# First mixture of experts: each expert's products in two halves of 32 slots, the second under a test

## The chip, the cores and the metric

The kernel runs on one core of a Trainium2 chip. The metric is the time of one execution on the device in microseconds (us), the median of three runs.

## The reference

The model has two layers over 256 context rows and 256 latent rows of width 1024. Each layer ends with a two-level mixture of 32 gated experts (width 512, float32). A token goes to two experts of one group of eight:

```python
grp = jnp.argmax(lg, axis=-1).astype(jnp.int32)
...
p_in, e_in = lax.top_k(jax.nn.softmax(le, axis=-1), MOE_TOP_K)
gates = gw * p_in / jnp.sum(p_in, axis=-1, keepdims=True)
eidx = grp[:, None] * MOE_PER_GROUP + e_in.astype(jnp.int32)
...
return (jax.nn.silu(xe @ w_gate[e]) * (xe @ w_up[e])) @ w_down[e]
```

The first layer's mixture takes all 512 rows, so 1024 pairs of a token and an expert, 32 per expert in the mean; the second layer's takes the 256 latent rows alone. For the inputs that are given, the reference's routing sends these numbers of tokens to the experts 0 to 31 of the first mixture: 41, 58, 58, 85, 39, 26, 53, 60, 17, 25, 20, 41, 18, 15, 44, 32, 17, 24, 27, 38, 29, 17, 18, 6, 30, 28, 21, 14, 45, 26, 24, 28. The kernel may not depend on them: any routing has to come out right.

## The kernel before, in words

Two functions compute a mixture: `experts()` (line 1895 on) the first, `narrow()` (line 2225 on) the second. In both, weights come through `Stream`, a ring of tiles of 128x2048 float32, 1 MB each: `take()` hands out the next tile, `give(n)` releases n and issues the next n loads on SP's queue (line 150). An expert has six tiles: gate and up for two halves of the inner dimension, then two of the down product. The ring has 11 slots in the first mixture (`RING`, line 24, the first two parts) and 16 in the second.

`experts()` goes through the experts in blocks of four (`GB`). The router makes a position for every pair; `onehot()` turns those of a block into selection matrices with 64 slots (`SLOTS`) per expert, and `gather()` brings the block's tokens into `XG`, one column per slot. Then for each expert e:

- `stage1` (line 1956), gate and up product: 16 pairs of matmuls into the bank b3. Gate uses 64 columns of the array, up the other 64, each with 512 columns of weights that stream past:

```python
for j in range(2):
    nc.tensor.matmul(ps[64 * j:64 * j + 64], xe(k), w[j][:, k % 4], start=k == 0, stop=k == 7)
```

- the test `tc.If(flag(e) > 0)` (flag line 2110, test line 2194): `shared()` (line 2042) is a further block for tokens beyond an expert's 64. Under expert 31's test lie also expert 0's and `others()`, a loop over blocks that could take any number of tokens beyond. The flags are computed on VectorE (`extra`) and read into a register by each engine.
- `hidden` (line 1958): silu of the gate half on ScalarE (line 1960), product with up half and gate weight on VectorE (line 1961).
- `products(e - 1)`: the down product of the expert before (`stage2`, line 1977), again two groups of 64 columns by 512, into b4; `parts` (line 1980) evacuates it in two pieces of 64x512, rounded by ScalarE (line 1984) and the rest by VectorE (line 1985). Then `give(6)`.
- scatter of finished pairs (`scatter`, line 1996; PE at line 2000), the gather of the next block, `hidden_t` (line 1966; four transposes at line 1969 and a copy), and for even e the turned selection matrix of a pair.

The profile counts two matmuls for each float32 one in the code. The order of the work is the order of this code on every engine: nothing reorders it. The second mixture (`narrow()`) has the same steps with 32 slots per expert (`NARROW`), gate and up product in four groups of 32 array columns by 256 columns of weights (line 2284), down product alike (line 2301), evacuation in four pieces (line 2449), a test of its own (line 2494), and down tiles loaded as two pieces of rows.

Of the kernel before, what the change touches and what calls it, by code (L numbers as in the profile page):

```python
# [206 lines left out]
class Kernel:  # L207
# [1404 lines left out]
    def moe_tiles(self, NT):  # L1612
# [8 lines left out]
            extra=mp.tile([128, NE + 1 if NT > 2 else 3 * NE + 1], I32, name="extra"))  # L1621
# [195 lines left out]
    def bookkeeping(self, gp, lgg, mg, m1, m2, ohg, masked, chosen, oh1, oh2, slots, blocks):  # L1817
# [33 lines left out]
        nc.vector.tensor_reduce(over, counts.rearrange("p t e -> p e t"), axis=AX.X, op=ALU.add)  # L1851
        nc.vector.tensor_scalar(over, over, float(slots), 0.0, op0=ALU.subtract, op1=ALU.max)
# [19 lines left out]
        flags = gp.tile([128, extra.shape[1]], F32, name="flags")  # L1872
# [13 lines left out]
        at = 0 if blocks > 1 else NE - 1  # L1886
        for v in (more, flags):
            nc.vector.tensor_tensor(flags[:, at:at + 1], flags[:, at:at + 1], v[:, 0:1], op=ALU.max)
# [7 lines left out]
    def experts(self, L, x, seg, bookkeeping, ending):  # L1896

        nc, tc, c, stream, I = self.nc, self.tc, self.c, self.stream, self.I
# [4 lines left out]
        GB = 4  # L1903
        with ExitStack() as st:
# [4 lines left out]

            place = cycle([(wp, "xg"), (self.xp, "x01")] if L else [(wp, "xg"), (wp, "xh")])  # L1910
# [28 lines left out]
            def gates_of(b):  # L1939

                g2 = self.m["gate2"]
                ps = pp.tile([128, GB // 2, 2, 2], F32, name="b2")
                for i in range(GB // 2):
                    for t in range(NT):
                        nc.tensor.matmul(ps[:, i].rearrange("p h e -> p (h e)"), OH[b][:, t, 2 * i:2 * i + 2].rearrange("p e s -> p (e s)"),
                                         g2[:, :, t, b * GB + 2 * i:b * GB + 2 * i + 2],
                                         start=i == 0 and t == 0, stop=t == NT - 1, skip_group_check=True)
# [10 lines left out]
            def hidden(ps, gs):  # L1958
                sg, hs = low[:, 0:FE], low[:, FE:].rearrange("p (k q) -> p k q", k=4)
                nc.scalar.activation(sg[64:128], ps[0:64], AF.Silu)  # L1960
                nc.vector.scalar_tensor_tensor(  # L1961
                    hs[64:128].rearrange("s k q -> s q k"), ps[64:128].rearrange("s (q k) -> s q k", k=4), gs,
                    sg[64:128].rearrange("s (q k) -> s q k", k=4), op0=ALU.mult, op1=ALU.mult)
                return hs

            def hidden_t(hs, ht, tag=dict(name="b2")):
                pt = pp.tile([128, 4, SLOTS], F32, **tag)
                for k in range(4):
                    nc.tensor.transpose(pt[:, k], hs[64:128, k], c["ident"][64:128, 64:128])
                ht = ht.rearrange("p (k s) -> p k s", k=4)  # L1970
# [3 lines left out]
            def stage2(ps, ht, w, half):  # L1974
                for k in range(2 * half, 2 * half + 2):
                    for j in range(2):
                        nc.tensor.matmul(ps[64 * j:64 * j + 64], ht[:, k], w[:, k % 2, 512 * j:512 * j + 512],  # L1977
                                         start=k == 0, stop=k == 3)

            def parts(ps, yh, yl):  # L1980

                for j in range(2):
                    pj = ps[64 * j:64 * j + 64]
                    nc.scalar.copy(out=yh[:, j], in_=pj)  # L1984
                    nc.vector.tensor_tensor(yl[:, j], pj, yh[:, j].bitcast(F32), op=ALU.subtract)  # L1985
# [56 lines left out]
            def shared(e, w):  # L2042

                ps = pp.tile([128, FE], F32, name="b7")
                for half in range(2):
                    stage1(ps, lambda k: xx[:, k], w(2 * half, 2), half)
                ht = hidden_t(hidden(ps, gx[64:128, e:e + 1]), wp.tile([128, 512], F32, name="tmp")[:, 0:256], dict(name="b7"))
                ps = pp.tile([128, 512], F32, name="b7")
                for half in range(2):
                    stage2(ps, ht, w(4 + half, 1)[0], half)  # L2050
# [3 lines left out]
            def back():  # L2054

                a, b = (xg(F32R) for i in range(2))
                oht = a[:, 0:T].rearrange("p (t q) -> p t q", t=NT)
                yh, yl = (v.rearrange("p (j f) -> p j f", j=2) for v in (a[:, T:T + 1024], b[:, 0:1024]))
                nc.scalar.copy(out=yh[0:64], in_=yx)
                nc.vector.tensor_tensor(yl[0:64], yx, yh[0:64].bitcast(F32), op=ALU.subtract)  # L2060
                turned(lambda t: ohx[:, t], SLOTS, oht)
                scatter([(oht, yh, SLOTS), (oht, yl, SLOTS)], pieces)
# [17 lines left out]
            def last_scatter(py, Y, OT):  # L2080

                bank = self.bank_of(("b0", "b1", "b5", "b6", "b7"))

                def scaled(s):
                    for i in range(2):
                        a = slice(64 * i, 64 * i + 64)
                        nc.vector.tensor_tensor(Y[s][64:128, i], py[a], g2[s][a, 512 * i:512 * i + 512], op=ALU.mult)

                scaled(segs[0])
                for t, j in pieces:  # L2090
                    s = seg[t]
                    if (t, j) == (0, 1) and segs[1:]:
                        scaled(segs[1])
                    ps = bank([128, 512])
                    nc.tensor.matmul(ps, OT[:, t].bitcast(F32), Y[s][:, j], start=True, stop=True)
# [4 lines left out]
            def load(e):  # L2100
                def get(at, n):
                    ws = [xg(F32) for i in range(n)]
                    for w, loads in zip(ws, self.expert_loads(L, e)[at:at + n]):
                        for view, src in loads:
                            nc.sync.dma_start(out=view(w), in_=src)
                    return [w.rearrange("p (k f) -> p k f", k=4 if at < 4 else 2) for w in ws]
                return get
# [4 lines left out]
            def others():  # L2112

                n = flag(NE, self.most_blocks(NT, 1))
                with tc.If(n > 0):
# [3 lines left out]
                    with tc.For_i(0, n, 1):  # L2119
# [3 lines left out]
                        for e in range(NE):  # L2123
                            shared(e, load(e))
                        back()
                    nc.gpsimd.memset(yx, 0.0)
# [4 lines left out]
            rest = bookkeeping(Carved(wp.tile([128, 1024], F32, name="yh")))  # L2131
# [5 lines left out]
            late = None  # L2137
            def products(e):

                ps = pp.tile([128, 512], F32, name="b4")  # L2140
                for half in range(2):
                    stage2(ps, ht[e], w[e][4 + half], half)
                if e + 1 < NE:
                    if e % 2 == 0:
                        y[e // 2] = [wp.tile([128, 2, 512], F32R, name=m) for m in ("yh", "yl")]
                    a = slice(64 * (e % 2), 64 * (e % 2) + 64)
                    parts(ps, *(v[a] for v in y[e // 2]))
# [437 lines left out]
```

## Time and profile before

| what | us |
|---|---|
| three runs | 1886.25, 1885.99, 1883.76 |
| median | 1885.99 |
| profiled execution, its own time | 1889.25 |
| its span in the trace | 1887.4 |
| PE (TensorE matmul) busy | 1636.5 (87%) |
| DVE (VectorE) busy | 817.7 (43%) |
| ACT (ScalarE) busy | 446.9 (24%) |
| POOL (GpSimd) busy | 139.3 (7%) |

The mean granted clock of TensorE over the span is 0.922 of full speed. The shares of busy time are means over stages with different limits; a change in one stage has to be read from that stage. SP issues the loads, and "PEq" or "SPq" is the sequencer of an engine, "PEld" TensorE's loading of weights beside its matmuls. PE, DVE and the like name the engines below. "w" is a tile of the ring, "b" a bank of the accumulator.

### The profile page before, as it was taken

How to read it: one execution, taken by the hardware profiler on the slowest of the kernel's cores; microseconds unless marked ns; L12 is line 12 of the kernel's file. 1: busy time of each engine (PE TensorE's matmuls, PEld its weight loads, DVE VectorE, ACT ScalarE, POOL GpSimd, SP SyncE). 2: the span in 40 equal slices, each digit the busy share in tenths (PEclk: the TensorE clock that was granted, in tenths of full speed). 3: DMA queues.
4: the chain of work that ended last, by engine and by line, in shares of the span. 5: the costliest groups of instructions: out<-in, count | busy, mean ns of one | idle time of the engine just before them, and what ended most of it. 6: DMA issues, size and time to landing. Idle time of an engine off the chain costs nothing. (4 is left out here: it accounts for less than half of the span.)

```text
span 1887.4 us, 31596 instructions
## 1 busy us (share of the span) xinstructions
PE 1636.5 (87%) x12946; PEld 930.7 (49%) x12946; DVE 817.7 (43%) x1622; ACT 446.9 (24%) x945; POOL 139.3 (7%) x169
## 2 busy tenths in 40 slices
PE   5988999989998999999999987999977887766665
PEld 2754556454775444444444434889743433332222
DVE  2455434644358245455555458564642212211112
ACT  3442222421113111111111114454421111111011
POOL 1111000102115000000000004100110000000000
PEclk8998988989898999999999998999999889888887
DMA  9266300643144879999999981522889998999992
GB/s 317 81 217 209 113 24 23 227 159 120 55 145 179 352 287 380 404 389 389 373 400 388 380 343 45 171 71 73 326 319 414 415 415 335 414 415 414 415 415 107
DMA packets 127284, 505.76 MB, mean 268 GB/s; under 512 B 11317, under 2 KB 38945, under 8 KB 85986
## 3 DMA queue, kind: packets, MB, share of 16 engines
q1 hardware_dynamic: 120946, 493.96, 67.4%
q0 software_dynamic: 3488, 8.26, 1.3%
q8 instruction: 144, 2.36, 0.5%
q10 hardware_dynamic: 2640, 0.65, 0.2%
q14 instruction: 66, 0.54, 0.1%
HBM read 501.73 MB, written 1.10 MB: 266 GB/s over the span
## 5 line engine op out<-in xcount | busy, mean ns | idle before, releaser
L1977 PE MATMUL b<-w,ht 128*64 128x512 f32 x512 | 118.5, 603 | 9.2 <-PEq L2194 8.3
L2002 DVE TENSOR_TENSOR tmp<-b,g 128x512 f32<-128x512 f32 x128 | 87.6, 686 | 70.1 <-PE b L2000 69.2
L1956 PE MATMUL b<-w,xh 128*64 128x512 f32 x512 | 117.0, 598 | 0.0
L1956 PE MATMUL b<-w,xg 128*64 128x512 f32 x512 | 116.9, 598 | 0.0
L2284 PE MATMUL b<-w,x 128*32 128x256 f32 x1024 | 80.3, 439 | 27.0 <-DMA w<-moe_w_up 21.5
L2301 PE MATMUL b<-w,ht 128*32 128x256 f32 x1024 | 78.3, 450 | 18.2 <-ACT ht L2296 13.3
L2284 PE MATMUL b<-w,xg 128*32 128x256 f32 x1024 | 73.7, 412 | 22.5 <-DMA w<-moe_w_up 13.6
L2004 DVE TENSOR_TENSOR x<-x,tmp 128x512 f32<-128x512 f32 x124 | 90.1, 726 | 4.3
L1985 DVE TENSOR_TENSOR yl<-b,yh 64x512 fp32r<-64x512 f32 x62 | 42.7, 688 | 101.7 <-ACT yh L1984 101.7
L2449 DVE COPY y<-b 32x256 f32<-32x256 f32 x62 | 25.9, 418 | 134.5 <-PE b L2301 121.2
L1977 PEld LDWEIGHTS b<-w,ht 128*64 128x64 f32 x512 | 41.5, 138 | 84.4 <-issue 69.1
L2289 DVE SCALAR_TENSOR_TENSOR low<-b,gs,low 64x256 f32<-64x256 f32 x32 | 15.7, 490 | 151.8 <-ACT low L2288 151.8
L1960 ACT ACTIVATE low<-b 64x512 f32<-64x512 f32 x33 | 19.4, 589 | 254.0 <-PEq L2194 232.8
L2284 PEld LDWEIGHTS b<-w,x 128*32 128x32 f32 x1024 | 37.4, 123 | 67.5 <-DMA w<-moe_w_up 29.8
L1984 ACT CAST yh<-b 64x512 fp32r<-64x512 f32 x62 | 36.0, 581 | 128.0 <-PE b L1977 104.7
L1961 DVE SCALAR_TENSOR_TENSOR low<-b,gs,low 64x512 f32<-64x512 f32 x32 | 36.1, 1127 | 67.3 <-ACT low L1960 67.3
L1956 PEld LDWEIGHTS b<-w,xh 128*64 128x64 f32 x512 | 34.3, 136 | 62.2 <-issue 61.7
L1956 PEld LDWEIGHTS b<-w,xg 128*64 128x64 f32 x512 | 33.9, 136 | 62.3 <-issue 61.3
L2284 PEld LDWEIGHTS b<-w,xg 128*32 128x32 f32 x1024 | 35.7, 119 | 57.1 <-DMA w<-moe_w_up 18.4
L2288 ACT ACTIVATE low<-b 64x256 f32<-64x256 f32 (+1 forms) x36 | 14.4, 400 | 204.5 <-PEq L2494 105.6
L2000 PE MATMUL b<-yh,oht 128*128 128x512 f32 (+1 forms) x128 | 57.9, 452 | 4.0 <-DVE tmp L2002 4.0
L1374 PE MATMUL b<-w,hH 128*128 128x256 f32 x320 | 60.9, 291 | 0.0
(865 smaller groups left out, 3101.3 us busy)
## 6 DMA issues: line engine op xcount, KB each, us to landing
w<-moe_w_gate SPq DMA_DIRECT2D x128, 1024.0 KB
w<-moe_w_up SPq DMA_DIRECT2D x128, 1024.0 KB
w<-moe_w_down SPq DMA_DIRECT2D x128, 1024.0 KB
w<-ada_w SPq DMA_DIRECT2D x48, 1024.0 KB
w<-od_w_in SPq DMA_DIRECT2D x12, 1024.0 KB
w<-ev_w_in SPq DMA_DIRECT2D x8, 1024.0 KB
w<-ev_w_out SPq DMA_DIRECT2D x5, 1024.0 KB
w<-od_w_out SPq DMA_DIRECT2D x4, 1024.0 KB
```

The costliest lines, as they stand in the source:

```text
L1374: nc.tensor.matmul(ps[:, t], l[:, k, T], r[:, k], start=t == 0 and k == 0 and i == 0, stop=k == 7 and i == 2, skip_group_check=True)
L1956: nc.tensor.matmul(ps[64 * j:64 * j + 64], xe(k), w[j][:, k % 4], start=k == 0, stop=k == 7)
L1961: nc.vector.scalar_tensor_tensor(hs[64:128].rearrange("s k q -> s q k"), ps[64:128].rearrange("s (q k) -> s q k", k=4), gs, sg[64:128].rea ...
L1977: nc.tensor.matmul(ps[64 * j:64 * j + 64], ht[:, k], w[:, k % 2, 512 * j:512 * j + 512], start=k == 0, stop=k == 3)
L1984: nc.scalar.copy(out=yh[:, j], in_=pj)
L1985: nc.vector.tensor_tensor(yl[:, j], pj, yh[:, j].bitcast(F32), op=ALU.subtract)
L2000: nc.tensor.matmul(ps, ohT[0:n, t], y[0:n, j], start=i == 0, stop=i == len(parts) - 1)
L2002: nc.vector.tensor_tensor(tmp, ps, g2[seg[t]][:, 512 * j:512 * j + 512], op=ALU.mult)
L2004: (nc.gpsimd if j in aside else nc.vector).tensor_tensor(xs, xs, tmp, op=ALU.add)
L2284: nc.tensor.matmul(ps[groups[j]], xe(k), w[j // 2][:, k % 4, 256 * (j % 2):256 * (j % 2) + 256], start=k == 0, stop=k == 7, skip_group_che ...
L2301: nc.tensor.matmul(ps[groups[j]], ht[:, k % 2, S * (k // 2):S * (k // 2) + S], w[:, k % 2, 256 * j:256 * j + 256], start=k == 0, stop=k == ...
L2449: (nc.scalar.copy if j % 2 else nc.vector.tensor_copy)(out=out, in_=ps[groups[j]])
```

## The change

Only the first mixture changes. `XG` and the selection matrices keep 64 slots per expert. Gate, up and down products are made for the first 32 slots of an expert in the four-group form of the second mixture. A second flag per expert, whether it has more than 32 tokens, stands in `extra`. Under a test of it the gate and up product of slots 32 to 63 are made into bank b7, then, nested, the old test and `shared()`; at the expert's end, under a second test of the same flag, comes that half's down product. The rows of a pair of experts are now two fixed pairs of tiles, set to zero at the start, since a half that is left out writes nothing. `give(6)` becomes `give(4)` behind the first test and `give(2)` behind the down product. Expert 0's test and `others()` move from expert 31 to expert 29. The down tiles come in two pieces of 4 KB per partition, as in the second mixture.

The diff, cut to its core:

```diff
-            [rows(I["moe_w_down"][L, e], 4, half) if L == 0 else
-             [(lambda w: w.rearrange("p (k f) -> p k f", k=2), I["moe_w_down"][L, e].rearrange("(k p) f -> p k f", k=4)[:, 2 * half:2 * half + 2])]
+            [[(lambda w: w.rearrange("p (k f) -> p k f", k=2), I["moe_w_down"][L, e].rearrange("(k p) f -> p k f", k=4)[:, 2 * half:2 * half + 2])]
              for half in range(2)]
...
+            nc.vector.tensor_scalar(flags[:, NE + 1:], over, NARROW + 0.5, None, op0=ALU.is_gt)
...
-                GS[b] = wp.tile([128, GB], F32, name="gs")
+                GS[b] = wp.tile([128, 2, GB], F32, name="gs")
                 for j in range(2):
-                    nc.vector.tensor_reduce(GS[b][64:128, j::2], ps[64 * j:64 * j + 64, :, :, j], axis=AX.X, op=ALU.add)
+                    for u in range(2):
+                        for h in groups[2:]:
+                            nc.vector.tensor_reduce(GS[b][h, u, j::2], ps[groups[2 * j + u], :, :, j], axis=AX.X, op=ALU.add)
...
                 for k in (4 * half + i for i in ks):
-                    for j in range(2):
-                        nc.tensor.matmul(ps[64 * j:64 * j + 64], xe(k), w[j][:, k % 4], start=k == 0, stop=k == 7)
+                    for j in range(4):
+                        nc.tensor.matmul(ps[groups[j]], xe(k), w[j // 2][:, k % 4, 256 * (j % 2):256 * (j % 2) + 256], start=k == 0, stop=k == 7,
+                                         skip_group_check=True)
...
+            def parts(ps, rows, yh, yl):
+
+                for j in range(4):
+                    out = slice(256 * (j % 2), 256 * (j % 2) + 256)
+                    nc.scalar.copy(out=yh[rows, j // 2, out], in_=ps[groups[j]])
+                    nc.vector.tensor_tensor(yl[rows, j // 2, out], ps[groups[j]], yh[rows, j // 2, out].bitcast(F32), op=ALU.subtract)
...
+            rows = [[wp.tile([128, 2, 512], F32R, name=f"y{m}{i}", bufs=1) for m in "hl"] for i in range(2)]
+            nc.gpsimd.memset(low, 0.0)
+            for y in sum(rows, []):
+                nc.scalar.copy(out=y.rearrange("p j f -> p (j f)"), in_=low)
...
+                if e == NE - 3:
+
+                    with tc.If(flag(0) > 0):
+                        shared(0, loaded(0))
+                        others()
                 for half in range(2) if e else ():
-                    stage1(ps, xe, w[e][2 * half:2 * half + 2], half)
+                    stage1(ps, xe(0), w[e][2 * half:2 * half + 2], half)
...
+                hs = hidden(ps, gs(0), low[64:128, 0:256], low[64:128, 256:512])
+                with tc.If(flag(NE + 1 + e) > 0):
+                    ps = pp.tile([128, 256], F32, name="b7")
+                    for half in range(2):
+                        stage1(ps, xe(1), w[e][2 * half:2 * half + 2], half)
+                    hidden(ps, gs(1), low[64:128, 512:768], low[64:128, 768:1024])
+                    if e:
+                        with tc.If(flag(e) > 0):
+                            shared(e, resident(w[e]))
+                if not end:
+                    stream.give(4)
                 if e:
-                    with tc.If(flag(e) > 0):
-                        shared(e, lambda at, n: w[e][at:at + n])
-                        if e + 1 == NE:
-                            with tc.If(flag(0) > 0):
-                                shared(0, load(0))
-                            others()
-                hs = hidden(ps, GS[b][64:128, r:r + 1])
-                if e:
-                    products(e - 1)
-                    if e + 1 < NE:
-                        stream.give(6)
+                    ps = second(e - 1, ht.pop(e - 1), w.pop(e - 1))
+                    parts(ps, *part_rows(e - 1, 0))
+                    if not end:
+                        stream.give(2)
                     scatter(rows_of(late) if todo else (), todo[n:])
...
+                with tc.If(flag(NE + 1 + e) > 0):
+                    ps = second(e, hidden_t(low[64:128, 768:1024], wp.tile([128, 512], F32, name="tmp")[:, 0:128].rearrange("p (k s) -> p k s", k=2)),
+                                w[e])
+                    if end:
+                        for s in segs:
+                            scaled(ps, s, 1)
+                    else:
+                        parts(ps, *part_rows(e, 1))
```

How the instructions stand on the engines. First PE around one expert's test, before. L1956 is the gate and up product, here its second half of 8 matmuls; the rows between the compare and the branches are `shared()`, and the L1977 row behind them is the down product of the expert before.

```order
L1956 MATMUL b_6668<-w,xg 64x512 x8
L2110 TENSOR_LOAD extra
L2194 COMPARE_AND_BRANCH
L1956 MATMUL b_6712<-w,xx 64x512 x16
L1969 MATMUL b_6732<-const_ident,low 128x64 x4
L1977 MATMUL b_6738<-w,tmp 64x512 x8
L2194 UNCONDITIONAL_BRANCH x2
L1977 MATMUL b_6751<-w,ht 64x512 x8
```

The same place now. L1961 is the gate and up product of 32 slots; the first compare (L2215) is the new flag's, the second (L2221) the old one's, nested in it.

```order
L1961 MATMUL b_7902<-w,xg 32x256 x16
L2123 TENSOR_LOAD extra
L2215 COMPARE_AND_BRANCH
L1961 MATMUL b_7964<-w,xg 32x256 x32
L2123 TENSOR_LOAD extra
L2221 COMPARE_AND_BRANCH
L2051 MATMUL b_8014<-w,xx 64x512 x16
L1972 MATMUL b_8036<-const_ident,tmp 128x64 x4
L2060 MATMUL b_8042<-w,tmp 64x512 x8
L2221 UNCONDITIONAL_BRANCH x2
L2215 UNCONDITIONAL_BRANCH
L1979 MATMUL b_8061<-w,ht 32x256 x16
```

The gate and up product of the second half has moved in ahead of the old test, and the old test is reached only where the new flag is set; behind the branches stands the down product of the expert before, now 16 matmuls of 32x256 instead of 8 of 64x512. At the expert's end PE has, behind rows of the selection matrix's transposes, this second test:

```order
L2123 TENSOR_LOAD extra
L2243 COMPARE_AND_BRANCH
L1972 MATMUL b_8148<-const_ident,low 128x64 x2
L1979 MATMUL b_8152<-w,tmp 32x256 x16
L2243 UNCONDITIONAL_BRANCH x2
L1961 MATMUL b_8177<-w,xg 32x256 x16
```

It holds the transposes of the second half's hidden rows and that half's down product, which before had no place of their own.

Second, ScalarE (ACT) ahead of the first mixture, before. L1740 rounds the rows of x, L1828 and L1829 are the router's exponentials, L1936 copies gathered tokens.

```order
L1740 CAST xh_4631<-VU_425 128x512 x2
L1828 ACTIVATE yh<-yh 128x16
L1829 ACTIVATE yh<-yh 128x4
L1936 COPY xg<-b_5105 128x512
L1936 COPY xg<-b_5123 128x512
```

And now:

```order
L1739 CAST xh_4631<-VU_425 128x512 x2
L2149 CAST yh_5080<-low 128x1024
L2149 CAST yl_5081<-low 128x1024
L2149 CAST yh_5082<-low 128x1024
L2149 CAST yl_5083<-low 128x1024
L1827 ACTIVATE xh<-xh 128x16
L1828 ACTIVATE xh<-xh 128x4
L1939 COPY xg<-b_5114 128x512
```

Four casts of 128x1024, the zeroing of the pair rows, have come in ahead of the exponentials.

Third, SP around a test, before. L2110 reads the flag, L150 issues a load.

```order
L2110 TENSOR_LOAD extra
L2110 ISA x2
L2194 COMPARE_AND_BRANCH
L2194 UNCONDITIONAL_BRANCH x2
L150 DMA w<-moe_w_up 128x2048
L150 DMA w<-moe_w_down 128x2048 x2
L150 DMA w<-moe_w_gate 128x2048
L150 DMA w<-moe_w_up 128x2048
L150 DMA w<-moe_w_gate 128x2048
```

And now (L2123 reads the flags):

```order
L2123 TENSOR_LOAD extra
L2123 ISA x2
L2215 COMPARE_AND_BRANCH
L2123 TENSOR_LOAD extra
L2123 ISA x2
L2221 COMPARE_AND_BRANCH
L2221 UNCONDITIONAL_BRANCH x2
L2215 UNCONDITIONAL_BRANCH
L150 DMA w<-moe_w_up 128x2048
L150 DMA w<-moe_w_down 128x2x1024 x2
L150 DMA w<-moe_w_gate 128x2048
L150 DMA w<-moe_w_up 128x2048
```

The nested test has come in ahead of the loads; the down loads have another shape. The rows that follow are the test at the expert's end (L2243), so that SP passes three tests for an expert where it passed one.

## Rows read from the trace of the kernel before

**Rows 1.** Windows of core 0, three of the first mixture, one of the second.

```profile
core 0: us, PE busy (x) PEld busy (x) DVE busy (x) ACT busy (x) POOL busy (x), PEclk, DMA share, GB/s
598.00:740.00 142.00, 136.60 (x706) 65.62 (x705) 54.68 (x113) 25.79 (x48) 0.00 (x0) 0.97 0.86 340
740.00:1080.00 340.00, 335.75 (x1686) 156.60 (x1688) 174.00 (x263) 62.04 (x116) 0.00 (x0) 1.00 0.98 392
1080.00:1166.00 86.00, 71.47 (x280) 30.25 (x277) 54.95 (x72) 18.02 (x38) 14.30 (x9) 0.90 0.51 204
...
1580.00:1840.00 260.00, 176.96 (x1918) 82.18 (x1913) 54.00 (x113) 30.11 (x85) 0.00 (x0) 0.88 1.02 413
```

**Rows 2.** Timeline of PE in the first mixture: start, duration, work [idle before].

```profile
740.05 3.65 PE L1977 MATMUL b<-w,ht 128*64 128x512 f32 x16 [0.16 <-PEq L2194]
...
804.71 3.65 PE L1977 MATMUL b<-w,ht 128*64 128x512 f32 x16 [0.16 <-PEq L2194]
...
812.67 3.65 PE L1956 MATMUL b<-w,xh 128*64 128x512 f32 x16
...
817.38 3.65 PE L1956 MATMUL b<-w,xh 128*64 128x512 f32 x16
...
1063.35 3.65 PE L1977 MATMUL b<-w,ht 128*64 128x512 f32 x16 [0.16 <-PEq L2194]
```

**Rows 3.** Waits of PE, 740 to 1080 us: us in total, times, longest us.

```profile
PE b L1977 <- DMA w<-moe_w_gate: 0.6, 2, 0.4
```

**Rows 4.** Waits of SP's own queue in the same stretch.

```profile
SPq L150 <- PEq L2194: 180.8, 18, 11.4
```

**Rows 5.** The page's list of loads (both mixtures: 2 x 64 gate loads).

```profile
w<-moe_w_gate SPq DMA_DIRECT2D x128, 1024.0 KB
```

**Rows 6.** Groups by line: busy us, mean ns | idle before, releaser.

```profile
L1985 DVE TENSOR_TENSOR yl<-b,yh 64x512 fp32r<-64x512 f32 x62 | 42.7, 688 | 101.7 <-ACT yh L1984 101.7
...
L1984 ACT CAST yh<-b 64x512 fp32r<-64x512 f32 x62 | 36.0, 581 | 128.0 <-PE b L1977 104.7 <-DVE yl L1985 23.2
...
L2449 DVE COPY y<-b 32x256 f32<-32x256 f32 x62 | 25.9, 418 | 134.5 <-PE b L2301 121.2 <-ACT y L2449 13.3
...
L2449 ACT COPY y<-b 32x256 f32<-32x256 f32 x62 | 22.6, 364 | 112.3 <-DVE y L2449 112.3
...
L1960 ACT ACTIVATE low<-b 64x512 f32<-64x512 f32 x33 | 19.4, 589 | 254.0 <-PEq L2194 232.8 <-PE b L1956 16.4 <-DVEq L2194 4.8
```

**Rows 7.** Timeline of PE, one expert of the second mixture.

```profile
1589.84 3.64 PE L2284 MATMUL b<-w,x 128*32 128x256 f32 x64
...
1595.00 0.31 PE L2295 MATMUL b<-const_ident,low 64*128 64x64 f32 x2 [1.52 <-PEq L2494]
...
1595.66 1.93 PE L2301 MATMUL b<-w,ht 128*32 128x256 f32 x32 [0.35 <-ACT ht L2296]
```

**Rows 8.** Line 2494, the second mixture's test: durations min/median/max ns; who waited (us, times).

```profile
L2494 PEldq COMPARE_BRANCH  x31: 70/350/5350, 1405.0 to 1864.8; - x31
...
  PE b L2262: 10.0, 8
...
  PE b L2295: 8.6, 3
...
  PE b L2316: 4.8, 7
```

**Rows 9.** Timeline of all engines around the first mixture's start.

```profile
582.56 1.04 ACT L1730 CAST xh<-VU 128x1024 fp32r<-128x1024 f32 x1 [3.83 <-DVE ss L1718]
...
594.53 0.94 POOL L2039 MEMSET low<- 64x1024 f32 x1
...
595.78 0.22 ACT L1828 ACTIVATE yh<-yh 128x16 f32<-128x16 f32 x1 [3.03 <-DVE e_m L1825]
...
598.74 0.59 ACT L1936 COPY xg<-b 128x512 f32<-128x512 f32 x1 [2.38 <-PE b L1933]
```

**Rows 10.** Timeline of PE, last expert of the first mixture.

```profile
1121.11 3.65 PE L1956 MATMUL b<-w,xh 128*64 128x512 f32 x16
...
1128.02 5.08 PE L1977 MATMUL b<-w,ht 128*64 128x512 f32 x16 [3.26 <-PEq L2194]
```

More of the change, by code (lines that the diff above doesn't have):

```diff
@@ L1902, in experts @@
         T = NT * 128
-        GB = 4
+        GB, S = 4, NARROW
+        groups = [slice(S * j, S * j + S) for j in range(4)]
         with ExitStack() as st:
@@ L2044, in shared @@
                 ps = pp.tile([128, FE], F32, name="b7")
-                for half in range(2):
-                    stage1(ps, lambda k: xx[:, k], w(2 * half, 2), half)
-                ht = hidden_t(hidden(ps, gx[64:128, e:e + 1]), wp.tile([128, 512], F32, name="tmp")[:, 0:256], dict(name="b7"))
+                for n in range(4):
+                    both = w(n)
+                    for k in range(2):
+                        for j, m in enumerate(both):
+                            nc.tensor.matmul(ps[64 * j:64 * j + 64], xx[:, 2 * n + k], m[:, k], start=n == 0 and k == 0, stop=n == 3 and k == 1)
+                sg, hs = (wp.tile([128, 512], F32, name="tmp")[64:128] for i in range(2))
+                hidden(ps, gx[64:128, e:e + 1], sg, hs)
+                ht = hidden_t(hs, wp.tile([128, 512], F32, name="tmp")[:, 0:256].rearrange("p (k s) -> p k s", k=4), 4, dict(name="b7"))
                 ps = pp.tile([128, 512], F32, name="b7")
                 for half in range(2):
-                    stage2(ps, ht, w(4 + half, 1)[0], half)
+                    down = w(4 + half)
+                    for k in range(2):
+                        for j in range(2):
+                            nc.tensor.matmul(ps[64 * j:64 * j + 64], ht[:, 2 * half + k], down[:, k, 512 * j:512 * j + 512],
+                                             start=half == 0 and k == 0, stop=half == 1 and k == 1)
                 for j in range(2):
@@ L2054, in back @@
             def back():
[L2056 to L2062, printed above, removed]
+                oht = turned(lambda t: ohx[:, t], SLOTS, wp.tile([128, 2048], F32, name="xg", bufs=1)[:, 0:T].rearrange("p (t q) -> p t q", t=NT),
+                             dict(name="b7"))
+                scatter([(oht, yx, SLOTS)], pieces)
             def last_tokens():
@@ L2098, in last_scatter, with loaded, piece, resident @@
                     ending(t, j)
[L2100 to L2107, printed above, removed]
+            def loaded(e):
+                def piece(n):
+                    w = wp.tile([128, 2048], F32, name="xg", bufs=1)
+                    for i in range(2):
+                        name, k = (("moe_w_gate", "moe_w_up")[i], 8) if n < 4 else ("moe_w_down", 4)
+                        src, a = self.I[name][L, e], slice(2 * n, 2 * n + 2) if n < 4 else slice(2 * (n - 4) + i, 2 * (n - 4) + i + 1)
+                        src = src.rearrange("(p k) f -> p k f" if n < 4 else "(k p) f -> p k f", k=k)[:, a]
+                        nc.sync.dma_start(out=w[:, 1024 * i:1024 * i + 1024].rearrange("p (k f) -> p k f", k=2 if n < 4 else 1), in_=src)
+                    w = w.rearrange("p (i k f) -> p i k f", i=2, k=2 if n < 4 else 1)
+                    return (w[:, 0], w[:, 1]) if n < 4 else w[:, :, 0]
+                return piece
+            def resident(w):
+                return lambda n: [m[:, 2 * (n % 2):2 * (n % 2) + 2] for m in w[2 * (n // 2):2 * (n // 2) + 2]] if n < 4 else w[n]
             def flag(e, most=1):
@@ L2123, in others @@
                         for e in range(NE):
-                            shared(e, load(e))
+                            shared(e, loaded(e))
                         back()
-                    nc.gpsimd.memset(yx, 0.0)
+                    for _ in block(None):
+                        pass
             pieces = [(t, j) for t in range(NT) for j in range(2)]
@@ L2136, in experts, with second, part_rows @@
             first = block(None)
[L2137 to L2140 removed]
+            def second(e, ht, w):
+                ps = pp.tile([128, 256], F32, name="b4")
                 for half in range(2):
[L2142 to L2149 removed]
+                    stage2(ps, ht, w[4 + half], half)
+                return ps
+            def part_rows(e, u):
+                return groups[2 * (e % 2) + u], *rows[e // 2 % 2]
             def rows_of(p, n=128):
[L2152 to L2156 removed]
+                return [(ohT[p], v, n) for v in rows[p % 2]]
+            w, ht, ohT = {}, {}, {}
             for e in range(NE):
@@ L2159, in experts @@
                 q = e % 2
+                end = e + 1 == NE
                 late = (e - 3) // 2
                 todo = pieces[NT * (1 - q):NT * (1 - q) + NT] if e >= 3 else []
[L2162 removed]
+                if end:
                     todo = pieces
```

98 lines of the change are left out of this document (44 added, 54 removed).

## The prediction

> **What bounds the kernel now.** I read the busy time by stretches first, then one expert on PE, then the waits of PE and of SP's queue, then the same product in the second mixture, which already has the new shape. The first mixture lies between 598 and 1166 us. In its steady part PE is busy 335.75 of 340 us at the full granted clock of 1.00, so 2.4 GHz, while DMA moves 392 GB/s; in the second mixture DMA moves 413 GB/s, with PE busy 177 of 260 us at a mean clock of 0.88 [rows 1]. So the first mixture is bound by PE, with only some 5% left before the loads bound it; the second is bound by its loads. The down product behind expert 7's test starts at 740.05 and the one behind expert 27's at 1063.35, so an expert takes 323.3 / 20 = 16.17 us [rows 2]; each gate/up half takes 3.65 us and the down product 3.65 us [rows 2]. In that part PE waits 0.6 us in all for a load [rows 3], and SP's queue of loads waits 180.8 us for PE to pass the test [rows 4]. An expert's six loads are 1024 KB each, 6.29 MB [rows 5]; at the 413 GB/s of the second mixture [rows 1] that is 15.2 us. That is the floor the change can reach, whatever it saves on PE.
>
> **How many experts pay.** The routing of these inputs gives eleven of 32 experts over 32 tokens: 0 to 4, 6, 7, 11, 14, 19, 28; only expert 3 has over 64. The trace agrees on the last: 33 silus, 32 and one of the shared block [rows 6]. So 21 experts skip the second half and eleven run it, seven of those among the first eight.
>
> **An expert that skips.** In the four-group form the gate/up product of one half takes 3.64 us and the down product 1.93 [rows 7]. PE saves 7.30 - 3.64 and 3.65 - 1.93, together 5.4 us. It gains one more test: a skipped one leaves PE idle for 0.16 us here [rows 2]; I take 0.3. The first test now jumps over a body about as long as that of the second mixture's test, where PE's branch takes 0.07 us at least, 0.35 in the median and 5.35 at most, and PE's three main waits behind it make 10.0 + 8.6 + 4.8 = 23.4 us over 31 tests, 0.8 each [rows 8]. I take 1.0 (bounds 0 and 5.3), as this is the same kind of jump at the same load on the queues. So PE needs 16.17 - 5.4 + 0.3 + 1.0 = 12.1 us, below the 15.2 of the loads.
>
> **An expert that runs both halves.** The products cost 2 x (3.64 + 1.93) = 11.1 us against 10.95. Beside them come two tests more (one nested), 0.2 us of further transposes, and in the second test PE waits for the copy of the transposed rows, 0.35 us as in the second mixture [rows 7], longer where the bank is still being read. I take +1.6 us in all; the bounds are +0.5 (the tests alone) and +3.
>
> **Work beside PE.** Evacuating a down product goes from two pairs of 0.58 us (ScalarE) and 0.69 us (VectorE) to four of 0.36 and 0.42: VectorE gains 0.3 us per half [rows 6], and it is busy 174 of 340 us [rows 1], so nothing. The gate reductions and the flag row are 0.2 us pieces on VectorE, nothing either; if that cover were gone they would cost some 1 us per four experts. The two-piece down loads are what the second mixture loads at 413 GB/s: nothing. SP now issues four of an expert's loads after the first test; in the steady part they already waited for the test [rows 4], so nothing. At expert 0 they go out later by a half product and a test, some 8 us, behind eight loads already queued, 8 x 2.5 us: nothing.
>
> **Start.** Four ScalarE casts of 128x1024 at 1.04 us stand ahead of the exponentials. The memset they wait for runs from 594.53 to 595.47, so they hold ScalarE until about 599.7, past the exponentials (595.78) and past the first gather copy (598.74) [rows 9]. The copy then starts near 600.1. Cost +1.5 us; at least 0, if the experts' start absorbs it, at most 4.2, all of the casts.
>
> **The sum,** against the profiled execution's own 1889.25 us (span 1887.4, 3.26 us over the median of the three runs):
> - start: +1.5.
> - experts 0 to 7: seven pay 1.6 and expert 5 saves 4.1, so +7.
> - from expert 7's test to the end of expert 31's gate/up: now 740.05 to 1121.11 + 3.65, 384.7 us [rows 2, 10]. PE would need 20 x 12.1 + 4 x 17.8 = 313 us, the loads more. The ring holds eleven, so at expert 7 the first 51 of the 192 are issued, and in the slow experts before it they have landed. Up to expert 31's last gate/up load 190 - 51 = 139 remain, 145.8 MB, 353 us at 413 GB/s. With 3 us from landing to product and 5 us for the four double experts that PE then catches up: 361, so -24.
> - end: the last test leaves PE idle 3.26 us and the next product runs at 5.08 us instead of 3.65, as the clock has fallen [rows 10]. The long jump over the overflow loop now stands at expert 29, where PE waits for loads anyway. I take -4 (bounds -6 and 0).
> - clock: PE, waiting for loads, will have a granted clock near the 0.88 of the second mixture [rows 1]. 12.1 / 0.88 = 13.8 is still under 15.2; for products run at 1.2 GHz at the end and behind stalls +3.
>
> Together 1.5 + 7 - 24 - 4 + 3 = -16.5: 1872.8 for the profiled execution, so about **1870 us** for the median.
>
> **Two rules of the skill.** The row shows that a jump in the second mixture can hold PE 5.35 us [rows 8]. The Trainium skill, Runtime: NRT & Kernel Launch, section Instruction fetch mechanics, says that a branch to code outside the pages held makes the engine wait for a fetch, and so speaks against a test per expert; by it all 21 skips could stall, which is the second rival. The trace agrees in part: the median is 0.35 us. The second mixture's clock of 0.88 means that about a quarter of the time is at 1.2 GHz [rows 1]. The Trainium skill, TensorE: Matmul & The Clock Gate, section HAM oscillation, says that short bursts of matmuls between waits for loads lose the fast clock every time; by it the whole second stretch could run slowly, which is the third rival. Here the trace agrees only for a quarter of the time.
>
> **Rivals.**
> - The loads bind earlier and nothing is lost: no stalls behind tests and no clock term, the second stretch at its floor of 353 + 3 us, the end at -6. For it speaks that the second mixture reaches 413 GB/s with stalls; against it the double experts. 1.5 + 5 - 29 - 6 = -28.5: 1858.
> - Slower: every skipped first test stalls 5.3 us. A skipping expert then takes 16.17 - 5.4 + 0.3 + 5.3 = 16.4 us, and the loads no longer matter. 20 x 0.2 + 4 x 1.6 + 1.5 + 11.4 - 4 = +19: 1905. It decides from 4.5 us on, where PE reaches 15.5 us. Against it stands the median of 0.35 [rows 8].
> - PE falls to a low clock. At a mean of 0.75 a skipping expert takes 12.1 / 0.75 = 16.1 us and the second stretch gains nothing beyond its end: 1.5 + 7 + 4 x 1.6 - 4 = +11, 1897; at 0.80 it takes 15.1 and some 2 us an expert are lost only around the double ones, 1882. The point is 0.79, where it crosses the loads' 15.2. For it speaks the 0.88 of a mixture with little work between its loads; against it that PE here works four fifths of the time.
> - The tests fire more often than the counts say (all 32): 32 x 1.6 + 1.5 = +53, 1939. Against it the counts.
>
> **Chances.** Forecast 0.64; first rival 0.13; low clock 0.14, of which 0.06 still faster, 0.05 level and 0.03 slower; stalls on every test 0.05; more tests 0.02; the forecast's own lower edge, where PE's double experts cost +3 each and the start 4.2, adds 12 us and stays faster. The remaining 0.02 I put on no effect. No change means within 0.2%, 3.8 us, about what a measurement can tell. Faster 0.64 + 0.13 + 0.06 = 0.83, same 0.07, slower 0.10. The range reaches from the first rival, 1858, to the low clock at 0.80 with a little over it, 1884.
>
> **What would show it.** In the profile of the changed kernel: DMA near 413 GB/s from expert 8 to 30, PE's products waiting for gate or up loads there, granted clock about 0.9; gate/up at 3.6 us per expert with one half; the last gate/up product ending near 1110 instead of 1124.8; 43 gate/up silus beside the shared one. Wrong would be: PE without waits for loads up to the end, branch times of several us behind most first tests, or a mean clock below 0.8.

## The result, and the profile after

The changed kernel takes 1909.50 us (median of four runs, 1902.45 to 1914.26) against 1884.97: ratio 1.0127, 95% interval 1.0092 to 1.0162. It is slower, where 1870 us and a gain were forecast. Its profiled execution took 1902.45 us (span 1900.7), 13.2 over that of the kernel before. Windows of the changed kernel, against [rows 1]:

```profile
598.00:740.00 142.00, 121.89 (x1510) 76.05 (x1510) 60.23 (x160) 34.20 (x88) 0.94 (x1) 0.99 0.78 307
740.00:1080.00 340.00, 280.15 (x3186) 176.45 (x3189) 189.64 (x376) 73.31 (x191) 0.00 (x0) 0.95 1.00 402
1080.00:1166.00 86.00, 55.60 (x512) 29.47 (x505) 47.38 (x77) 15.40 (x38) 15.40 (x11) 0.79 0.58 224
```

PE is busy for 280 instead of 336 us in the steady part, as forecast, but DMA reaches 402 GB/s there instead of 413, and before 740 us it falls from 340 to 307. The timeline of PE shows the first down product behind the tests of experts 1, 7, 28, 29 and 31, with expert 29's gate/up product behind the long jump among them (L1961), and the start of the mixture's last down product, against [rows 2, 10]. The long jump is the skipped test over expert 0's block and the overflow loop:

```profile
634.62 1.93 PE L1979 MATMUL b<-w,ht 128*32 128x256 f32 x32 [0.46 <-PEq L2221]
...
753.78 1.93 PE L1979 MATMUL b<-w,ht 128*32 128x256 f32 x32 [0.63 <-PEq L2221]
...
1082.85 1.93 PE L1979 MATMUL b<-w,ht 128*32 128x256 f32 x32 [0.58 <-DMA w<-moe_w_gate]
...
1098.23 3.64 PE L1961 MATMUL b<-w,xh 128*32 128x256 f32 x32 [4.29 <-PEq L2205]
...
1110.14 3.32 PE L1979 MATMUL b<-w,ht 128*32 128x256 f32 x32 [2.67 <-PEq L2215]
...
1138.28 1.93 PE L1979 MATMUL b<-w,ht 128*32 128x256 f32 x32 [1.06 <-PEq L2215]
...
1149.18 3.64 PE L1979 MATMUL b<-w,ht 128*32 128x256 f32 x32 [3.17 <-DVEq L2243]
```

I compare the same marks in the traces: an expert's mark is the start of the first down product behind its test. The origin is the router's first group test on VectorE (595.46 us before), since what lies ahead of it moves by up to 12 us between executions of programs that are alike there. Lengths in us; the last column is the mixture from origin to last down product.

| kernel | to expert 7's mark | 7 to 28 | 28 to 31 | mixture |
|---|---|---|---|---|
| before | 144.6 | 339.8 | 48.2 | 542.6 |
| changed, profiled | 159.8 | 329.1 | 55.4 | 555.2 |
| changed again (e7) | 163.2 | 335.2 | 57.1 | 566.3 |
| e3, no tests, no second halves | 112.8 | 320.9 | 50.7 | 493.6 |
| e10, wide or narrow | 142.6 | 321.0 | 58.2 | 534.3 |
| e14, best | 145.2 | 332.8 | 42.8 | 532.8 |

Two executions of the changed kernel differ by 11 us in the mixture alone; the 1902.45 of the profiled one is the fastest of its four. So the first eight experts lose 15 to 19 us, the next 21 gain 5 to 11, and the last stretch, with the long jump at expert 29, loses 7 to 9. Each row rests on one trace; that of e10 is of the fastest of its twelve executions (1875.16 us).

### The profile page after: what moved, and what is told of

It reads as the page before. It is cut to its first block, busy times and chain, and to the rows that moved or that the text cites. A ratio compares the mean times of both kernels' runs of the same rounds, so it can differ in the third digit from the quotient of the medians.

```text
span 1900.7 us, 37966 instructions
## 1 busy us (share of the span) xinstructions
PE 1567.0 (82%) x15496; PEld 965.3 (51%) x15496; DVE 837.0 (44%) x1792; ACT 471.9 (25%) x1077; POOL 141.2 (7%) x172
## 5 line engine op out<-in xcount | busy, mean ns | idle before, releaser
L1987 DVE TENSOR_TENSOR yl<-b,yh 32x256 fp32r<-32x256 f32 x168 | 70.6, 420 | 170.7 <-ACT yh L1986 170.2
L1979 PE MATMUL b<-w,ht 128*32 128x256 f32 x1024 | 73.2, 413 | 53.0 <-issue 19.2
L1986 ACT CAST yh<-b 32x256 fp32r<-32x256 f32 x168 | 61.0, 363 | 197.2 <-PE b L1979 134.0
L2338 PE MATMUL b<-w,ht 128*32 128x256 f32 x1024 | 87.8, 487 | 20.0 <-ACT ht L2333 13.1
L2321 PE MATMUL b<-w,x 128*32 128x256 f32 x1024 | 79.9, 431 | 25.2 <-DMA w<-moe_w_up 19.6
L1961 PE MATMUL b<-w,xg 128*32 128x256 f32 x1408 | 86.2, 382 | 8.7 <-DMA w<-moe_w_up 4.3
L2321 PE MATMUL b<-w,xg 128*32 128x256 f32 x1024 | 74.7, 420 | 19.6 <-DMA w<-moe_w_up 11.8
L1961 PE MATMUL b<-w,xh 128*32 128x256 f32 x1344 | 82.1, 389 | 7.4 <-PEq L2205 4.3
L1979 PEld LDWEIGHTS b<-w,ht 128*32 128x32 f32 x1024 | 37.5, 116 | 87.0 <-issue 45.6
L1961 PEld LDWEIGHTS b<-w,xg 128*32 128x32 f32 x1408 | 45.4, 110 | 42.0 <-issue 10.7
L2338 PEld LDWEIGHTS b<-w,ht 128*32 128x32 f32 x1024 | 36.7, 133 | 55.1 <-issue 26.6
L2321 PEld LDWEIGHTS b<-w,xg 128*32 128x32 f32 x1024 | 36.3, 121 | 55.1 <-DMA w<-moe_w_up 16.5
L1961 PEld LDWEIGHTS b<-w,xh 128*32 128x32 f32 x1344 | 44.4, 112 | 38.9 <-issue 16.0
L1965 ACT ACTIVATE low<-b 64x256 f32<-64x256 f32 x43 | 16.1, 375 | 176.3 <-PE b L1961 110.1
```

What stands on the lines that cost most here:

```text
L1961: nc.tensor.matmul(ps[groups[j]], xe(k), w[j // 2][:, k % 4, 256 * (j % 2):256 * (j % 2) + 256], start=k == 0, stop=k == 7, skip_group_che ...
L1965: nc.scalar.activation(sg, ps[0:64], AF.Silu)
L1979: nc.tensor.matmul(ps[groups[j]], ht[:, k % 2, S * (k // 2):S * (k // 2) + S], w[:, k % 2, 256 * j:256 * j + 256], start=k == 0, stop=k == ...
L1986: nc.scalar.copy(out=yh[rows, j // 2, out], in_=ps[groups[j]])
L1987: nc.vector.tensor_tensor(yl[rows, j // 2, out], ps[groups[j]], yh[rows, j // 2, out].bitcast(F32), op=ALU.subtract)
L2321: nc.tensor.matmul(ps[groups[j]], xe(k), w[j // 2][:, k % 4, 256 * (j % 2):256 * (j % 2) + 256], start=k == 0, stop=k == 7, skip_group_che ...
```

## The experiments

**The floor, and the tests (e2, e3, e8).** e2, with the test's place moved as in e1:

```diff
-            nc.vector.tensor_scalar(flags[:, NE + 1:], over, NARROW + 0.5, None, op0=ALU.is_gt)
+            nc.vector.tensor_scalar(flags[:, NE + 1:], over, 1000.5, None, op0=ALU.is_gt)
```

e2, e3 and e8 leave out all tokens over an expert's 32nd. e3 drops both `tc.If(flag(NE + 1 + e) > 0)` blocks of e2 from the program; e8 drops only `tc.If(flag(e) > 0)` and `shared(...)` from the first of them.

> As e1_others_at_31, with the bound of the new flag at 1000 tokens instead of 32, so that every test of a second half is there and is skipped; the tokens 33 on of an expert are left out of the result. Theory A: PE needs about 12 us an expert, stalls included, and the loads (15.2 us an expert) bind from the first expert on: the last gate and up product ends near 1075 instead of 1125 us, 1830 to 1845 in all. Theory B: each of 32 skipped tests stops PE for 3 us or more, an expert takes 15 to 16.4 us, and the run is at 1870 or above.

> As e2_never_second, with the two tests of an expert and what they hold taken out of the program: the same work is done, without any jump but the one at expert 31. Theory A: the loads bind in both, so within 4 us of e2_never_second. Theory B: faster than e2_never_second by 1 us or more for each of the 32 experts, 30 us and more.

> As e2_never_second (1858), without the nested overflow test and block in the body of the first test: the jump goes over 32 matmuls instead of 32 + 28 and a second test. The overflow block of expert 3 is left out, which e2_never_second skips as well. If PE's stops behind the first test (median 0.42 us, up to 4.3 us there in the changed kernel) come of the length of the jump, the median branch time of PE falls to that of the second test (0.2 us) and the run is 5 to 15 us faster than e2_never_second; if any jump costs the same, within 4 us of it.

Measured: e2 1858.30 us (ratio 0.9835, 0.9808 to 0.9861), e3 1834.62 (0.9722, 0.9696 to 0.9747), e8 1852.83 (0.9809, 0.9788 to 0.9830). In e3 the loads bind from expert 4 on, 15.3 us an expert from 7 to 28. Its windows:

```profile
600.00:740.00 140.00, 114.94 (x1226) 72.28 (x1224) 68.93 (x153) 30.81 (x75) 0.00 (x0) 0.96 1.02 416
740.00:1040.00 300.00, 243.97 (x2482) 144.67 (x2482) 159.42 (x311) 56.03 (x144) 0.00 (x0) 0.94 1.02 416
```

So the floor of the forecast is there. e2 is 24 us above it with the same work, against both theories: more than theory A's 4, less than theory B's 30. In the two traces the mixture differs by 19.4 us, of which 7.2 lie ahead of expert 2's mark and 11.7 between the marks of 2 and 28. PE's branch at the first test (durations in ns: least/median/most) in e2:

```profile
L2215 PEldq COMPARE_BRANCH  x32: 241/1264/6177, 612.3 to 1095.5; - x32
```

The same in e8, with the short body:

```profile
L2215 PEldq COMPARE_BRANCH  x32: 207/325/1976, 611.2 to 1088.0; - x32
```

The longer body goes with longer stops: 1264 against 325 ns. Also, PE stands over 2 us in the middle of a product seven times in e2's trace, 22.7 us in all, with no releaser in the profile ("issue"); in e8, in e3 and in the kernel before it never does. But length alone does not set the branch: the second mixture's test is over two blocks like the nested one, 56 matmuls, and its median is 350 ns [rows 8]. The Trainium skill, Runtime: NRT & Kernel Launch, section Instruction fetch mechanics, says that a branch out of the pages held waits for a fetch; these rows fit that, but none of them names a fetch. The time that e8 gains, 5.5 us, has overlapping intervals.

**What a double expert costs (e4, e6).** e4 is e1 with both tests of the second halves taken away and their bodies always run. e6 is e5 with `stage1`, `stage2` and `parts` of the kernel before for e < 8:

```diff
+                        nc.tensor.matmul(ps[64 * j:64 * j + 64], xe(k), w[j][:, k % 4], start=k == 0, stop=k == 7)
...
+                wd = e < WIDE
+                ps = pp.tile([128, 512 if wd else 256], F32, name="b3")
```

> As e1_others_at_31, with the tests of the second halves taken out and both halves always done (the old test of the overflow block stays). It tells what two halves cost without tests. The price of a double expert in the first eight of the changed kernel was 2.0 to 2.7 us over the kernel before. If that is waits for copies and short products (theory A's view), all 32 experts pay about 1.5 to 2 us and the run is at 1930 to 1950; if it is the tests (theory B), they pay 0.5 and the run is at 1895 to 1905.

> As e5_overflow_loads_on_pool, with experts 0 to 7 in the form of the kernel before (64 slots at once, two groups of 64 columns, one test), the other 24 in halves under tests. Seven of those eight run both halves in the changed kernel, at 16 to 17 us each after the first where DMA stands at 307 GB/s. If the double experts are what the first eight lose (13.7 us at expert 7's test), this run is 11 to 15 us faster than e5_overflow_loads_on_pool, and with the stretch behind it still bound by its loads it ends at 1873 to 1887, below the kernel before. If they lose it to the start (casts, the flags' arrival at SP), under 5 us faster.

e4: 1969.44 us (1.0430, 1.0400 to 1.0461), 81 us over the kernel before on that chip, above both expectations. In its steady part (marks of experts 12 to 27) an expert takes 17.88 us against 16.14. Its timeline shows one expert from its first down product to the next one's, 18.64 us, with the half's product waiting for its transposed rows:

```profile
822.41 1.93 PE L1979 MATMUL b<-w,ht 128*32 128x256 f32 x32 [0.18 <-PEq L2220]
...
827.76 0.34 PE L1972 MATMUL b<-const_ident,low 64*128 64x64 f32 x2
829.65 1.93 PE L1979 MATMUL b<-w,tmp 128*32 128x256 f32 x32 [1.55 <-ACT tmp L1973]
...
835.49 5.39 PE L1961 MATMUL b<-w,xh 128*32 128x256 f32 x96
841.05 2.35 PE L1979 MATMUL b<-w,ht 128*32 128x256 f32 x32 [0.18 <-PEq L2220]
```

So without these tests a double expert costs 1.7 us more than before in the steady part, near the 1.6 of the sum. That is not all of the 81 us: of the 79 by which the mixture's trace is longer, 54 lie ahead of expert 28's mark and 25 behind it (83.4 against 58.2 us), where the end was not taken apart. e6: 1891.88 us (1.0019, 1.0002 to 1.0037), 21 us under e5, more than the 11 to 15 expected, but not down to the 1887 forecast; its mark of expert 7 stands 144.0 us behind the origin, as before. The loss in the first eight is the double experts with their tests, not the casts.

**The long jump (e1, e5, e13).** e1 puts `if e == NE - 3:` back to `NE - 1`; e5 changes one word; e13 is e5 with the test at `e == 20`, ahead of `onehot`:

```diff
-                        nc.sync.dma_start(out=w[:, 1024 * i:1024 * i + 1024]
+                        nc.gpsimd.dma_start(out=w[:, 1024 * i:1024 * i + 1024]
```

> The changed kernel with expert 0's test and the overflow loop's test moved back from expert 29 to expert 31 (there ahead of the expert's gate and up product), and nothing else. Theory A, loads drained: in the changed kernel SP leaves the skipped test of expert 29 only after every load in flight has landed (1089.4 to 1104.1 us) and DMA stands still for some 10 us. By it this run is 9 to 13 us faster than the changed kernel (1909.5), so 1897 to 1900, with DMA above 390 GB/s up to the last load of expert 31. Theory B, stalls behind tests: the time went to PE's own stops behind the skipped tests of the second halves (3 to 4 us each in the middle of a product), and the long jump only changes its place: under 4 us faster, 1906 to 1909.

> The changed kernel with one word changed: the loads inside the overflow test at expert 29 (which is never taken here) are issued by GpSimd instead of SP, so that SP's way past that test has no load of SP's kind in it and no wait for the loads in flight at its end. Theory A (drain): SP passes expert 29's test within 1 us plus a fetch, DMA does not fall to zero around it, and the run is 8 to 12 us faster than e7_changed_again. Theory B: the drain only took time that PE lost anyway, under 3 us.

> The changed kernel itself, on this chip beside the others: 1902 to 1914, ratio to before 1.009 to 1.016, in the trace again a stop of the loads of about 10 us behind expert 29's test.

> The changed kernel with that test at expert 20 and its loads on GpSimd, nothing else. If the stop is covered: expert 20's iteration grows by 2 to 6 us, experts 21 to 23 give it back, iteration 29 falls from 27 to some 15 us, and the run is 7 to 12 us faster than e7_changed_again (1907.4): 1895 to 1900. If it is lost anywhere: 1904 or above.

e1 1904.01 us (1.0080, 1.0057 to 1.0104), e5 1913.21 (1.0144, 1.0127 to 1.0161), e7 1907.41 (1.0115, 1.0089 to 1.0140), e13 1910.16 (1.0110, 1.0081 to 1.0138). Moved back to expert 31 the jump gains 3.4 us on e7 by the medians, with overlapping intervals; the two others gain nothing. The drain theory, that SP's wait for the loads in flight is what costs the time, has fallen. In the changed kernel SP does wait at that test for the loads in flight (its waits, 1080 to 1115 us), in all 14.3 us:

```profile
SPq L2205 <- SPq L2205: 14.3, 5, 5.2
```

and DMA stops, as its windows show:

```profile
1090.00:1095.00 5.00, 3.64 (x32) 1.38 (x32) 1.36 (x3) 0.76 (x3) 0.00 (x0) 0.50 1.03 420
...
1100.00:1105.00 5.00, 3.87 (x28) 1.77 (x21) 0.69 (x1) 0.00 (x0) 0.00 (x0) 0.50 0.35 139
1105.00:1110.00 5.00, 2.48 (x33) 1.05 (x32) 2.48 (x4) 0.38 (x1) 0.00 (x0) 0.84 0.02 3
```

In e5 SP is past the test at 1085.8 us, and still issues nothing from 1083.65 to 1106.57, since the tiles come free only when PE passes the next test. DMA stops there too:

```profile
1100.00:1105.00 5.00, 4.36 (x36) 1.92 (x35) 2.76 (x5) 0.38 (x1) 0.00 (x0) 0.66 0.02 3
```

PE is what stands. Its branch there in e5:

```profile
L2205 PEldq COMPARE_BRANCH  x1: 5951/5951/5951, 1088.2 to 1088.2; - x1
```

SP's issues around it, in e5's timeline:

```profile
1083.65 0.43 SPq L150 DMA_DIRECT2D w<-moe_w_gate  x1
1106.57 0.34 SPq L150 DMA_DIRECT2D w<-moe_w_up  x1
```

And PE's two halves of expert 29's gate/up product behind it:

```profile
1094.45 3.64 PE L1961 MATMUL b<-w,xh 128*32 128x256 f32 x32 [4.35 <-PEq L2205]
...
1101.53 2.83 PE L1961 MATMUL b<-w,xh 128*32 128x256 f32 x32
```

The stop of 5.95 us is followed by a product at twice its 1.93 us. In the changed kernel the granted clock there is 0.50, and it had fallen before the jump: in the window from 1090 us PE is busy with expert 28's second down product alone, 3.64 us instead of 1.93, behind waits of 1.9 and 0.7 us for ScalarE. In e13 the iteration of expert 20 takes 25.2 instead of 17.0 us, experts 21 to 23 give little back (40.0 against 41.5 us in e7), and the end is 6 us shorter: a stop of that length is lost at either place, as far as two traces tell.

**The length of the jump in the change itself (e9).** The nested test moves behind the block that holds it:

```diff
-                    if e:
-                        with tc.If(flag(e) > 0):
-                            shared(e, resident(w[e]))
+                if e:
+                    with tc.If(flag(e) > 0):
+                        shared(e, resident(w[e]))
```

> The changed kernel with the overflow test of an expert taken out of the body of the second half's test and put behind it: one test more for an expert, every jump shorter (about 30 matmuls each). With never-taken tests the shorter body saved 5.5 us over 32 experts. If the length of the jump sets PE's stop, here 21 of 32 experts skip: the median stop of PE at a skipped first test falls to about 0.3 us and the run is 2 to 5 us faster than e7_changed_again (1907.4). If the number of tests counts, it is 3 us or more slower, as there are 31 more of them.

1907.08 us (1.0103, 1.0067 to 1.0140): level with e7. PE's branch at the first test falls to a median of 187 ns, that of the test behind it has 222, and four stops in the middle of products are left; the time meets neither expectation. Shorter jumps and one test more may cancel; that is not shown.

**Versions that might beat both (e10, e11, e12, e14).** e10 has, for experts 1 to 30,

```diff
+                    with tc.If(flag(NE + 1 + e) > 0) as cmp:
+                        ps = pp.tile([128, 512], F32, name="b3")
+                        for half in range(2):
+                            stage1w(ps, xw, w[e][2 * half:2 * half + 2], half)
...
+                    with cmp.Else():
+                        ps = pp.tile([128, 256], F32, name="b3")
+                        for half in range(2):
+                            stage1(ps, xe(0), w[e][2 * half:2 * half + 2], half)
```

and the same for the down product, with the overflow test alone behind it, the tiles given back six at a time as before and the long jump at expert 31; e11 joins e6, e9 and e1, without e5's word; e12 and e14 are e10 and e11 with e13's place of the long jump.

> A version that is to beat both: under the flag an expert with over 32 tokens runs in the form of the kernel before (64 slots at once, two groups of 64 columns), else in 32 slots and four groups of 32 columns; the same for the down product; the overflow test stands alone, so that no jump is over more than some 30 matmuls; experts 0 and 31 have a fixed form; expert 0's test and the overflow loop's are at expert 31. If the double experts (2 us over the kernel before each, 11 of them) and the long jumps are what the change loses, the first eight experts take as long as before, the rest is bound by its loads at 15.2 to 15.5 us an expert, and the run is at 1868 to 1878 (ratio 0.990 to 0.995). If three jumps an expert stop PE by 1 us or more each, it is level with the kernel before or slower, 1885 to 1900.

> e6_wide_first_eight (1891.9, level with the kernel before) with the overflow test not nested and expert 0's test at expert 31 instead of 29. From the runs so far the place at 31 is worth 3 to 5 us and the shorter jump 2 to 5 us: 1882 to 1887, ratio 0.997 to 0.9995. If both only move the stops to another place, 1889 or above.

> e10_wide_or_narrow (1886, level with the kernel before) with expert 0's test and the overflow loop's at expert 20 and its loads on GpSimd, so that the long jump stands where eight experts of loads follow and SP does not wait for loads in flight. If the stop of 4 to 7 us is covered there by the loads behind it, expert 30's and 31's iterations fall from 18.6 and 22.7 us to some 15 and the run is 6 to 12 us faster than e10: 1874 to 1880. If a stop of that length is lost anywhere, it is within 3 us of e10.

> e11_wide_eight_short_jumps (1882.9) with that test at expert 20 and its loads on GpSimd. If the stop is covered there, the end of the mixture (iterations 30 and 31, 13.7 and 26.1 us) loses 8 us or more and the run is at 1871 to 1878, clearly below the kernel before; if not, within 3 us of e11.

e10 1886.11 us (0.9995, 0.9971 to 1.0019), e11 1882.86 (0.9987, 0.9967 to 1.0008), e12 1882.65 (0.9967, 0.9944 to 0.9990), e14 1877.81 (0.9945, 0.9924 to 0.9967). e12 and e14 beat both kernels, the kernel before by 0.3 and 0.5%. e11 and e14 came as expected; e10 missed its 1868 to 1878, and e12 lies between its two expectations. e10's stretch from expert 7 to 28 is 321.0 us with four double experts, the 320.9 of e3: in that trace, with double experts in the wide form and short jumps, the loads' floor is reached. Its end gives much back: PE stands 9.30 us between expert 31's gate/up product and the down product behind the long jump, 4.3 of them in that jump's branch, and 28 to 31 takes 58.2 us. At expert 20 the jump still lengthens that iteration to 23 us in e12 and e14, but their end falls to 49.6 and 42.8 us. e14 rests on the first eight experts being large, which is so for this routing; e12 asks the counts.

## Why the prediction was wrong

- **How many experts pay:** right. Silus of a gate/up product in the page's groups: 11 + 32.

```profile
L1965 ACT ACTIVATE low<-b 64x256 f32<-64x256 f32 x43 | 16.1, 375 | 176.3 <-PE b L1961 110.1
```

- **An expert that skips:** the products are as forecast (gate/up in two halves of 1.93, down product 1.93 us), and a skipping expert behind a late one takes 12.3 us (expert 21), as the 12.1 said. But the stop is not 1 us each. PE's waits from 634 to 1150 us have 15.3 us behind the first test and 19.2 us in the middle of down products, 34.5 / 21 = 1.6 us for each skip by estimate:

```profile
PE b L1979 <- issue: 19.2, 6, 4.3
PE b L1979 <- PEq L2215: 15.3, 11, 3.7
```

Expert 5, forecast to save 4.1 us, saved 1.7, and gave some 2.7 back behind its test:

```profile
715.28 1.24 PE L1979 MATMUL b<-w,ht 128*32 128x256 f32 x17 [0.48 <-PEq L2215]
719.98 1.50 PE L1979 MATMUL b<-w,ht 128*32 128x256 f32 x15 [3.47 <-issue]
```

- **An expert that runs both halves:** +1.6 was right without tests (1.7 in e4). With them experts 2 to 4 cost 2.0, 2.0 and 2.7 more than before. The start was near: +3.8 at expert 1's mark, double experts 0 and 1 in it. By these sizes and expert 5's the first eight came to +15 to +19 instead of +8.5.
- **From expert 7's test to expert 31's gate/up, the step that failed most:** 361 us forecast, 1137.22 - 753.78 = 383.4 measured, against 384.7 before. Of the 361, e3's pace gives 321 to the stretch up to expert 28's mark and so 40 to the rest; measured were 329.1 and 54.4, the rest before 44.9. So 8 of the 22 us that are missing lie ahead of that mark (14 in e7) and 14 behind it, where expert 29's iteration alone takes 27.3 us instead of 15.2 (16.9 in e1, with the jump at expert 31). The floor was right; the step "5 us for the four double experts that PE then catches up" was not, nor that the long jump at expert 29 costs nothing "where PE waits for loads anyway". The forecast let PE's slack of 3 us an expert add up. The ring holds eleven tiles and an expert uses six, so five loads, 5 x 2.5 us, are ahead: a double expert of 18 to 20 us with a stop behind or before it empties them, and what DMA then stands idle does not come back. Experts 7 to 28 took 329 to 335 us against the floor's 321, and the stretch with the long jump took 7 to 9 more than before, with PE's stop and products at half rate in it. That experts 7 to 28 take 321.0 in e10 shows that the loads did not keep them up. How double experts and stops share this is open: e11, with experts 11, 14 and 19 still in halves, takes 323.3, and e6, with long bodies too, 326.0, while e9, whose bodies alone are short, takes 332.5. By these single traces most of it goes with the form of the first eight, though it is lost behind expert 7's mark; why is not shown. A deeper ring was not tried, so the share of its depth is argued, not shown.
- **End:** -4 forecast, 12.0 against 13.3 us from the last gate/up product to the last down product: -1.3.
- **Clock:** 0.95 in the steady part instead of the 0.88 taken, 0.82 from expert 28's mark to 31's. Products run at down to half their rate behind stops of some 3 to 4 us (15 matmuls in 1.50 us behind 3.47, the last down product in 3.64 us behind 3.17). What this cost in all was not measured, so no run shows the +3. The Trainium skill, TensorE: Matmul & The Clock Gate, section HAM oscillation, tells of a kernel whose waits for loads are longer than its bursts of matmuls, and which loses the fast clock at every tile. PE busy for 280 of 340 us, at 0.95, is another case; the third rival did not come.
- **The rivals:** "every skipped first test stalls 5.3 us" gave 1905 us, nearly the time, by another mechanism: the median of PE's branch at all 33 recorded first tests is 0.42 us.

```profile
L2215 PEldq COMPARE_BRANCH  x33: 70/422/4327, 610.5 to 1136.2; - x33
```

## What to carry to other kernels

Compare a test per item not with the mean work saved, but item by item with what the buffers ahead can cover: savings under a floor are lost at once, while every item above it and every stop is paid. Give the frequent large case its old efficient form instead of two runs of the small one, keep the body of a test short (its stops shrink; a gain in time was not shown for it alone), and don't put a jump over a huge body into a stretch that has only an item's buffers ahead. A floor is best measured by a run without tests before the sum relies on it.

## What was not expected of the hardware

A block that is skipped but holds loads made SP wait at its end for every load in flight (14.3 us), and with the loads on another engine that wait vanished without a gain, because PE's 5.95 us stop behind the same jump ended last. And one program's mixture took 555 us in one profiled execution and 566 in another, with the stops behind its tests in other places: differences of 5 us between such kernels need more than single traces.
